# Two-block transformer on one core: recurrence outputs in another PSUM bank, decay moved onto the keys, masked diagonal copies, and sparse-attention operands loaded two heads earlier

## The chip, the cores and the metric

The program runs on one core of a Trainium2 chip. A core has five engines with a queue each: TensorE (PE, with its weight loads as PEld), VectorE (DVE), ScalarE (ACT), GpSimd (POOL) and SyncE (SP), which here issues nearly all DMAs. Each queue runs in the order in which the program put the instructions. The metric is device time in microseconds (us), the median of several executions.

## The reference

512 tokens of width 1024 pass two blocks in float32. Block 1 is attention over two blocks of 256 tokens with a causal mask and a distance bias, a pooling branch and an MLP. Block 2 has a mixer with two branches: an RWKV-7 recurrence and a sparse attention (NSA) with 16 query heads in 4 groups. A gate merges the branches; cross attention and a convolutional MLP follow. Two pieces matter here:

```python
def step(state, inp):                       # rwkv7_scan, 16 heads of 64
    r_t, w_t, k_t, v_t, a_t, b_t = inp
    sa = jnp.einsum('bhvk,bhk->bhv', state, a_t)
    state = state * w_t[:, :, None, :] + sa[..., None] * b_t[:, :, None, :] + v_t[..., None] * k_t[:, :, None, :]
    return state, jnp.einsum('bhvk,bhk->bhv', state, r_t)
...
out = gb[..., 0:1] * o_c + gb[..., 1:2] * o_s + gb[..., 2:3] * o_w    # NSA: compressed, selected, window
```

## The kernel before, in words

All matrices are kept with features on partitions and 512 tokens along the free axis. A float32 product is made of three passes over operands split into a high and a low part (lines 242 to 244), or of plain float32 matmuls, which the profile shows as two records each.

The part that the change touches is the stage between the projections and the merge of the two branches, from about 1050 to 1530 us of the span. `emit` weaves three instruction streams there (`weave`, with the weights 190, 240 and 65 for their pace), and a scheduler then fixes the order on every engine:

- stream "" is `nsa`: 4 groups, each with a prologue (load the group's queries, keys and bias, split them, scores against the compressed keys at L1124, a softmax over them, lines 1125 to 1147) and then 4 heads with two branches each through `attend` (scores L307/L308, exponentials L311, scaling L317/L319, transposes L324, evictions L326/L327, products L328/L329).
- stream "_b" is `rwkv_backs`: for 8 pairs of heads, `rwkv_operands` prepares a pair (keys transposed at L827 and copied to `L3` at L828, values at L833, inverse blocks at L843 and L849) while `rwkv_chain` walks the 8 chunks of 64 tokens of the pair before it, and `rwkv_finish` normalises its output.
- stream "_m" is `merge_gates`: 10 column tiles of a projection (buffer `psg_m`), with 512 KB weight tiles loaded at L208, split at L221 and L222, and sent to memory by POOL at L954.

A step of `rwkv_chain` is a sequence of dependent pieces, each of two heads on the diagonal of a 128x128 block. In one PSUM bank, tile `p` (`psb_b` in the profile) has four blocks of 128 columns: the state against the chunk (`p[:, 1]`, L868), copied by DVE to `RH` (L870, one copy for each head); the output of the chunk before (`p[:, 0]`, L873 and L875), copied by ACT to `Y` (L877); the solved values (`p[:, 2]`, L882), copied by DVE to `VU` (L884); the state's increment (`p[:, 3]`, L886), which DVE adds to the decayed state (L893), where ACT has put state times decay ahead of it (L892). The bank has one buffer, and waits are kept for the tile as a whole.

`ld` is a pool of three 128x512 buffers through which the sparse attention loads values, keys, queries and the compressed bias (L292, L1100, L1110, L1115); `f` has three buffers as well, `kb` one, and PSUM bank 5 (`psa_b`) serves `rwkv_operands` alone.

Of the kernel before, what the change touches and what calls it, by code (L numbers as in the profile page):

```python
# [38 lines left out]
class Gen:  # L39
# [248 lines left out]
    def k_stack(self, k, par):  # L288

        t = self.f("ld")  # L290
        for b in range(2):
            self.nc.sync.dma_start(t[64 * b:64 * b + 64], k[64 * par:64 * par + 64])  # L292
        return self.split(t, tag="kst")
# [327 lines left out]
    def rwkv_state(self):  # L621
# [6 lines left out]
        self.ne, self.et = (zero(n, 512).rearrange("p (c t) -> p c t", c=4) for n in ("ne", "et"))  # L628
        self.cen = zero("cen", 128)
# [163 lines left out]
    def rwkv_operands(self, pr):  # L793
# [29 lines left out]

        for q in range(2):
# [31 lines left out]
    def rwkv_chain(self, pr, out, L3, VS, VU, YI):  # L856
# [8 lines left out]
        for c in range(9):  # L865
            p = self.ps("b").rearrange("p (e n) -> p e n", e=4)
            if c < 8:
                nc.tensor.matmul(p[:, 1], fl(L1[:, c]), fl(VS[:, c]), start=True, stop=True)  # L868
                for a in H:
                    V.tensor_copy(RH[a, a], p[a, 1, a])  # L870
            if c:

                nc.tensor.matmul(p[:, 0], fl(VU[:, c - 1]), L4[:, :, c - 1], start=True, stop=c == 1)  # L873
                if c > 1:
                    nc.tensor.matmul(p[:, 0], fl(VS[:, c - 1]), self.rb[:, :, c - 1], start=False, stop=True)  # L875
                for a in H:
                    S.copy(Y[a, c - 1], p[a, 0, a])  # L877
# [5 lines left out]
            for h, a in enumerate(H):  # L883
                V.tensor_copy(VU[a, c, h], p[a, 2, a])  # L884
            if c < 7:
                nc.tensor.matmul(p[:, 3], L3[:, c], fl(VU[:, c]), start=True, stop=True)  # L886
                d = self.decay[:, pr, c:c + 1]
                for h, a in enumerate(H):
                    if c == 0:
                        V.tensor_scalar(VS[a, 1, h], p[a, 3, a], d[a], None, op0=OP.mult)  # L890
                    else:
                        S.activation(VS[a, c + 1, h], VS[a, c, h], AF.Copy, scale=d[a])  # L892
                        V.scalar_tensor_tensor(VS[a, c + 1, h], p[a, 3, a], d[a], VS[a, c + 1, h], OP.mult, OP.add)  # L893
# [140 lines left out]
    def nsa(self):  # L1034

        nc, A, V, S = self.nc, self.A, self.nc.vector, self.nc.scalar
        for gp in range(2):
            yield from self.nsa_groups(gp, *self.cmp)

# [54 lines left out]
    def nsa_groups(self, gp, kc, vc):  # L1094
# [9 lines left out]
        for gl in range(2):  # L1104
            g = 2 * gp + gl
            kst = {br: self.k_stack(self.kvd[2 + 2 * br + gp], gl) for br in (1, 2)}
            qst = {}
            for i in range(2):
                q = self.f("ld")
                nc.sync.dma_start(q, self.qd[2 * g + i])  # L1110
                for par in range(2):
                    qst[2 * i + par] = self.q_stack(q, par, -0.125)

            cb = self.f("ld")
            nc.sync.dma_start(cb, bass.AP(tensor=self.gfd.tensor, offset=self.gfd.offset + 4 * g * 1056 + 513,  # L1115
# [477 lines left out]
```

## Time and profile before

| | |
|---|---|
| median of 3 runs | 2163.73 us (2156.9 to 2164.24) |
| the profiled execution's own time | 2160.68 us |
| its span, first to last instruction | 2158.9 us |
| instructions | 28062 |
| busy PE / PEld / DVE / ACT / POOL | 2040.6 / 1640.7 / 1333.7 / 957.7 / 64.1 us |
| mean granted TensorE clock | 0.969 |
| HBM traffic | 205.12 MB read, 45.53 MB written |

PE is called busy for 95% of the span. A share over the span hides that the stages differ: in the dense products PE runs without a gap, and in the woven stage it doesn't. A row of the waits names the engine and line that stood idle, and the engine and line that ended the wait; the three numbers are the sum, the count and the longest. The granted clock is 1.00 at 2.4 GHz and 0.50 at 1.2 GHz; a stretch in between had both.

### The profile page before, as it was taken

Reading aid. Unit: us, or ns where it says so; the run is one execution under the profiler, and the core shown is the slowest. Engines: PE = TensorE matmul, PEld = TensorE weight load, DVE = VectorE, ACT = ScalarE, POOL = GpSimd, SP = SyncE. Lnnn points to the kernel's source line nnn. Section 1 sums busy time; section 2 is a strip of 40 time slices with the busy share of each in tenths; the row PEclk is TensorE's granted clock in tenths of the full one; section 3 lists DMA queues with packets and bytes.
Section 4 is the critical chain, followed back from the end, with each engine's and each line's share of the span. In section 5 each row is a group of like instructions: output and inputs, shape, how many; then the busy total and the mean of one; then the engine's idle time right before and its main releaser. Section 6 shows DMA issues by size and latency. Waiting matters only on the chain.

```text
span 2158.9 us, 28062 instructions
## 1 busy us (share of the span) xinstructions
PE 2040.6 (95%) x9927; PEld 1640.7 (76%) x9927; DVE 1333.7 (62%) x3111; ACT 957.7 (44%) x1874; POOL 64.1 (3%) x131
## 2 busy tenths in 40 slices
PE   8999999999999999899888997887999999999999
PEld 7777888888887778677676776665778878888887
DVE  5785433553556576969388877775656766666522
ACT  4864422442343243333376776765424443333311
POOL 0000000000011201000000000000000000000000
PEclk9999999999999999999999998997999999999999
DMA  4233233333465756455544544351543122333332
GB/s 160 74 93 97 89 98 94 116 109 121 130 203 157 175 149 167 146 147 165 167 106 115 137 115 114 101 157 59 161 151 89 59 69 88 98 98 90 98 113 81
DMA packets 172493, 256.71 MB, mean 119 GB/s; under 512 B 87200, under 2 KB 102768, under 8 KB 172352
## 3 DMA queue, kind: packets, MB, share of 16 engines
q1 hardware_dynamic: 169024, 244.42, 38.8%
q0 software_dynamic: 3328, 10.49, 1.4%
q8 instruction: 79, 1.29, 0.3%
q14 instruction: 62, 0.51, 0.1%
HBM read 205.12 MB, written 45.53 MB: 116 GB/s over the span
## 4 chain that ended last, share of the span: by engine, by line
PE 43%; DVE 7%; DMA 5%; ACT 3%; issue 1%; SPq 0%; ACTq 0%; DVEq 0%
PE psg L244 8%; PE psg L242 8%; PE psg L243 8%; PE psg_b L243 1%; PE psg_b L244 1%; PE psg_b L242 1%; DMA bias<-grd 1%; DVE ys L772 1%; DMA ws<-in_w_in 1%; PE psg_p L242 1%; PE psb L324 1%; PE psg_p L243 1%; PE psg_p L244 1%; DMA ld<-qd 1%; PE psa L739 1%
## 5 line engine op out<-in xcount | busy, mean ns | idle before, releaser
L221 ACT CAST wh<-ws 128x1024 fp32r<-128x1024 f32 (+2 forms) x283 | 291.5, 1031 | 707.3 <-PE psg L243 461.1
L222 DVE TENSOR_TENSOR wl<-ws,wh 128x1024 fp32r<-128x1024 f32 (+2 forms) x283 | 340.2, 1203 | 275.1 <-ACT wh L221 269.8
L242 PE MATMUL psg<-xh,wh 128*128 128x512 f32 x984 | 392.8, 399 | 4.6 <-ACT wh L221 4.6
L244 PE MATMUL psg<-xh,wl 128*128 128x512 f32 x984 | 393.7, 400 | 0.0
L243 PE MATMUL psg<-act,wh 128*128 128x512 f32 x912 | 360.3, 395 | 1.1 <-DVE act L165 1.1
L242 PEld LDWEIGHTS psg<-xh,wh 128*128 128x128 f32 x984 | 186.0, 189 | 46.7 <-ACT wh L221 5.4
L244 PEld LDWEIGHTS psg<-xh,wl 128*128 128x128 f32 x984 | 186.1, 189 | 41.9 <-issue 1.2
L243 PEld LDWEIGHTS psg<-act,wh 128*128 128x128 f32 x912 | 171.5, 188 | 43.0 <-DVE act L165 1.5
L242 PE MATMUL psg<-act,wh 128*128 128x512 f32 x496 | 196.6, 398 | 2.8 <-ACT act L164 1.4
L244 PE MATMUL psg<-act,wl 128*128 128x512 f32 x496 | 196.7, 397 | 0.5 <-DVE wl L222 0.5
L243 PE MATMUL psg<-xl,wh 128*128 128x512 f32 x352 | 139.7, 397 | 0.0
L242 PEld LDWEIGHTS psg<-act,wh 128*128 128x128 f32 x496 | 93.2, 188 | 27.4 <-ACT act L164 2.2
L244 PEld LDWEIGHTS psg<-act,wl 128*128 128x128 f32 x496 | 93.4, 188 | 23.9 <-DVE wl L222 1.3
L311 ACT ACTIVATE p<-p,sm 128x128 f32<-128x128 f32 (+3 forms) x160 | 89.5, 560 | 18.1 <-DVE sm L309 16.7
L243 PE MATMUL psg<-x,wh 128*128 128x512 f32 x216 | 88.9, 412 | 0.0
L327 DVE TENSOR_TENSOR pt<-psb,pt 128x512 fp32r<-128x512 f32 (+3 forms) x160 | 76.4, 489 | 19.3 <-ACT pt L326 16.2
L324 PE MATMUL psb<-ident,p 128*128 128x128 f32 x400 | 80.8, 293 | 2.9 <-DVE y L917 1.2
L309 DVE CUSTOM_DVE_ANT_0 p<-psa,bias 128x128 f32<-128x128 f32 (+3 forms) x160 | 76.0, 487 | 11.4 <-PE psa L308 4.9
L326 ACT CAST pt<-psb 128x512 fp32r<-128x512 f32 (+3 forms) x160 | 66.2, 423 | 33.9 <-PE psb L324 31.1
L243 PEld LDWEIGHTS psg<-xl,wh 128*128 128x128 f32 x352 | 66.2, 188 | 14.3
L242 PE MATMUL psg_p<-xh,wh 128*128 128x512 f32 x176 | 72.8, 414 | 0.8 <-ACT f L953 0.6
L243 PE MATMUL psg_p<-x,wh 128*128 128x512 f32 x176 | 72.3, 411 | 0.0
(485 smaller groups left out, 3944.4 us busy)
## 6 DMA issues: line engine op xcount, KB each, us to landing
ws<-in_w_in SPq DMA_DIRECT2D x59, 512.0 KB, 4.3
ws<-in_w_fup SPq DMA_DIRECT2D x44, 512.0 KB, 3.4
ws<-in_w_up SPq DMA_DIRECT2D x32, 512.0 KB, 3.6
ws<-in_w_down SPq DMA_DIRECT2D x32, 512.0 KB, 3.6
ws<-in_w_fdn SPq DMA_DIRECT2D x16, 512.0 KB, 3.5
ws<-in_w_qku SPq DMA_DIRECT2D x12, 512.0 KB, 3.3
ws<-in_w_out SPq DMA_DIRECT2D x8, 512.0 KB, 3.6
ws<-in_w_cak SPq DMA_DIRECT2D x8, 512.0 KB, 4.3
```

Of the source, the lines that this page charges most:

```text
L221: nc.scalar.copy(wh[:, :n], ws[:, :n])
L222: nc.vector.tensor_tensor(wl[:, :n], ws[:, :n], wh[:, :n].bitcast(F32), OP.subtract)
L242: nc.tensor.matmul(p[:, :n], wh[:, s], h[:, :n], start=c + k == 0, stop=False)
L243: nc.tensor.matmul(p[:, :n], wh[:, s], l[:, :n], start=False, stop=False)
L244: nc.tensor.matmul(p[:, :n], wl[:, s], h[:, :n], start=False, stop=last)
L309: nc.vector.tensor_tensor_reduce(pt, ps[:, :w], bias[:, 512 - w:], 1.0, 3e38, OP.add, OP.min, m[:, i:i + 1])
L311: nc.scalar.activation(pt, pt, AF.Exp, bias=m[:, i:i + 1], scale=-1.0, accum_out=s[:, i:i + 1])
L324: nc.tensor.transpose(ps[:, (i - j) * 128:(i - j + 1) * 128], P[i][:, j * 128:j * 128 + 128], self.ident)
L326: nc.scalar.copy(ph[:, :w], ps[:, :w])
L327: nc.vector.tensor_tensor(pl[:, :w], ps[:, :w], ph[:, :w].bitcast(F32), OP.subtract)
L739: nc.tensor.matmul(p[:, c], KB[hs, 4 * q + c].rearrange("p e t -> p (e t)"), AR[hs, :, 4 * q + c], start=True, stop=True)
L772: V.tensor_tensor(q, a, Y[:, :n, :t + 1], OP.mult)
```

## The change

- `rwkv_chain` writes the output of the chunk before into a tile of its own from `self.ps("a")`, which for this stream is bank 5, and ACT copies `Y` from there.
- The two DVE copies for the heads become one `copy_predicated` over 128 columns, for `RH` and for `VU`; the mask `diag` is the block matrix `blk` read as integers.
- `rwkv_operands` multiplies the keys `KB` (128x1024) by the decay of their chunk on POOL, ahead of the transposes. The product of L886 then comes out decayed, ACT's multiplication (L892) is gone, and one DVE instruction for each head makes state times decay plus increment.
- `nsa_loads` takes the loads of a group's two query tiles, its compressed bias (now in an `f` buffer) and the keys of its first branch out of the prologue. For groups 1 to 3 it is called when the third head of the group before begins (`h == 2`), for group 0 at the start. The keys of the second branch and the values are loaded where they were.

```diff
--- before.py
+++ after.py
@@ -285,12 +285,15 @@
         nc.vector.scalar_tensor_tensor(st[b], q[a], scale, st[a].bitcast(F32), OP.mult, OP.subtract)
         return st
 
-    def k_stack(self, k, par):
-
+    def k_load(self, k, par):
         t = self.f("ld")
         for b in range(2):
             self.nc.sync.dma_start(t[64 * b:64 * b + 64], k[64 * par:64 * par + 64])
-        return self.split(t, tag="kst")
+        return t
+
+    def k_stack(self, k, par):
+
+        return self.split(self.k_load(k, par), tag="kst")
 
     def attend(self, qst, kst, bias, V, o, first, last, gate=None):
 
@@ -626,6 +629,7 @@
         self.yi = [zero(f"yi{i}", 1024).rearrange("p (c h t) -> p c h t", c=8, h=2) for i in range(2)]
         self.rh = zero("rh", 128)
         self.ne, self.et = (zero(n, 512).rearrange("p (c t) -> p c t", c=4) for n in ("ne", "et"))
+        self.diag = self.blk.rearrange("p a b -> p (a b)").bitcast(I32)
         self.cen = zero("cen", 128)
         for t in (*self.yi, self.rh, self.ne, self.et, self.cen):
             nc.gpsimd.memset(t, 0.0)
@@ -821,6 +825,7 @@
             nc.gpsimd.memset(VS[64 * h:64 * h + 64, 0, h], 0.0)
         yield 1.0
 
+        nc.gpsimd.tensor_tensor(KB, KB, self.decay[:, pr][:, :, None].to_broadcast([128, 8, 128]), OP.mult)
         for q in range(2):
             p = self.ps("a")
             for c in range(4):
@@ -866,31 +871,29 @@
             p = self.ps("b").rearrange("p (e n) -> p e n", e=4)
             if c < 8:
                 nc.tensor.matmul(p[:, 1], fl(L1[:, c]), fl(VS[:, c]), start=True, stop=True)
+                V.copy_predicated(RH, self.diag, p[:, 1])
+            if c:
+
+                o = self.ps("a")
+                nc.tensor.matmul(o[:, :128], fl(VU[:, c - 1]), L4[:, :, c - 1], start=True, stop=c == 1)
+                if c > 1:
+                    nc.tensor.matmul(o[:, :128], fl(VS[:, c - 1]), self.rb[:, :, c - 1], start=False, stop=True)
                 for a in H:
-                    V.tensor_copy(RH[a, a], p[a, 1, a])
-            if c:
-
-                nc.tensor.matmul(p[:, 0], fl(VU[:, c - 1]), L4[:, :, c - 1], start=True, stop=c == 1)
-                if c > 1:
-                    nc.tensor.matmul(p[:, 0], fl(VS[:, c - 1]), self.rb[:, :, c - 1], start=False, stop=True)
-                for a in H:
-                    S.copy(Y[a, c - 1], p[a, 0, a])
+                    S.copy(Y[a, c - 1], o[a, a])
             if c in (4, 8) and pr < 7:
                 self.rwkv_load(pr + 1, c // 8)
             if c == 8:
                 break
             nc.tensor.matmul(p[:, 2], fl(YI[:, c]), RH, start=True, stop=True)
-            for h, a in enumerate(H):
-                V.tensor_copy(VU[a, c, h], p[a, 2, a])
+            V.copy_predicated(fl(VU[:, c]), self.diag, p[:, 2])
             if c < 7:
                 nc.tensor.matmul(p[:, 3], L3[:, c], fl(VU[:, c]), start=True, stop=True)
                 d = self.decay[:, pr, c:c + 1]
                 for h, a in enumerate(H):
                     if c == 0:
-                        V.tensor_scalar(VS[a, 1, h], p[a, 3, a], d[a], None, op0=OP.mult)
+                        V.tensor_copy(VS[a, 1, h], p[a, 3, a])
                     else:
-                        S.activation(VS[a, c + 1, h], VS[a, c, h], AF.Copy, scale=d[a])
-                        V.scalar_tensor_tensor(VS[a, c + 1, h], p[a, 3, a], d[a], VS[a, c + 1, h], OP.mult, OP.add)
+                        V.scalar_tensor_tensor(VS[a, c + 1, h], VS[a, c, h], d[a], p[a, 3, a], OP.mult, OP.add)
             yield 1.2
         g, bv = self.f("vgb"), self.f("vgb")
         nc.sync.dma_start(g, self.vgd[pr, 1])
@@ -1034,8 +1037,21 @@
     def nsa(self):
 
         nc, A, V, S = self.nc, self.A, self.nc.vector, self.nc.scalar
+        self.ahead = self.nsa_loads(0)
         for gp in range(2):
             yield from self.nsa_groups(gp, *self.cmp)
+
+    def nsa_loads(self, g):
+
+        nc = self.nc
+        qs = []
+        for i in range(2):
+            qs.append(self.f("ld"))
+            nc.sync.dma_start(qs[i], self.qd[2 * g + i])
+        cb = self.f("f")
+        nc.sync.dma_start(cb, bass.AP(tensor=self.gfd.tensor, offset=self.gfd.offset + 4 * g * 1056 + 513,
+                                      ap=[[1056, 4], [-16, 32], [1, 512]]))
+        return qs, cb, self.k_load(self.kvd[4 + g // 2], g % 2)
 
     def nsa_compressed(self):
         nc, A, V, S = self.nc, self.A, self.nc.vector, self.nc.scalar
@@ -1103,17 +1119,10 @@
             V.tensor_tensor(v[:, :, :, 64:128], z, v[:, :, :, 0:64].bitcast(F32), OP.subtract)
         for gl in range(2):
             g = 2 * gp + gl
-            kst = {br: self.k_stack(self.kvd[2 + 2 * br + gp], gl) for br in (1, 2)}
-            qst = {}
-            for i in range(2):
-                q = self.f("ld")
-                nc.sync.dma_start(q, self.qd[2 * g + i])
-                for par in range(2):
-                    qst[2 * i + par] = self.q_stack(q, par, -0.125)
-
-            cb = self.f("ld")
-            nc.sync.dma_start(cb, bass.AP(tensor=self.gfd.tensor, offset=self.gfd.offset + 4 * g * 1056 + 513,
-                                          ap=[[1056, 4], [-16, 32], [1, 512]]))
+            qs, cb, k1 = self.ahead
+            qst = {2 * i + par: self.q_stack(qs[i], par, -0.125) for i in range(2) for par in range(2)}
+            kst = {1: self.split(k1, tag="kst"), 2: self.k_stack(self.kvd[6 + gp], gl)}
+
             kz = self.f("kz", F32R, (128, 448)).rearrange("p (i n) -> p i n", i=2)
             nc.gpsimd.memset(kz.bitcast(F32), 0.0)
             for i, k in enumerate(kc):
@@ -1153,6 +1162,8 @@
                 par = h % 2
                 if par == 0:
                     O = self.f("o")
+                if h == 2 and g < 3:
+                    self.ahead = self.nsa_loads(g + 1)
                 bias = self.f("bias")
                 nc.sync.dma_start(bias, bass.AP(tensor=self.grd.tensor, offset=self.grd.offset + hd * 1280 + 127,
                                                 ap=[[576, 2], [-1, 64], [1, 512]]))
```

The scheduler orders the three streams anew. PE at the last chunks of the eighth pair, in the kernel before (`psb_b` is the chain's bank, `kst` keys, `pt` transposed probabilities):

```order
L329 MATMUL pso_13328<-pt_13534,vt_11591 128x512
L324 MATMUL psb_13549<-ident,p_13501 128x128 x2
L868 MATMUL psb_b_13307<-vs_12580,ws_9002 128x128
L873 MATMUL psb_b_13307<-wh_9003,vu_12581 128x128
L875 MATMUL psb_b_13307<-rb,vs_12580 128x128
L882 MATMUL psb_b_13307<-rh,yi_5055 128x128
L886 MATMUL psb_b_13307<-vu_12581,bk_12579 128x128
L868 MATMUL psb_b_13397<-vs_12580,ws_9002 128x128
L873 MATMUL psb_b_13397<-wh_9003,vu_12581 128x128
```

The same place in the changed kernel (`psa_b` is bank 5, `psg_m` the merge gates; L873, L887 and L890 are the former L868, L882 and L886):

```order
L873 MATMUL psb_b_13248<-vs_12474,ws_9002 128x128
L332 MATMUL pso_13179<-pt_13243,vt_11521 128x128
L311 MATMUL psa_13431<-kst_12750,qst_12743 128x256
L310 MATMUL psa_13436<-kst_12749,qst_12743 128x384
L311 MATMUL psa_13436<-kst_12750,qst_12743 128x384
L887 MATMUL psb_b_13248<-rh,yi_5055 128x128
L244 MATMUL psg_m_13630<-xh_4697,wl_13634 128x512
L310 MATMUL psa_13441<-kst_12749,qst_12743 128x512
L327 MATMUL psb_13376<-ident,p_13349 128x128
L890 MATMUL psb_b_13248<-vu_12475,bk_12473 128x128
L878 MATMUL psa_b_13264<-wh_9003,vu_12475 128x128
```

Before, the chain's matmuls of these chunks follow each other; now matmuls of the attention and of the gates stand between them, and the output (L878) comes behind the chain's last matmul of the step.

SP at the loads of the third group, in the kernel before (`yi`, `vu`, `ynd` are other streams' transfers):

```order
L811 DMA yi_5055<-ydr 32x8x32 x4
L1110 DMA ld_11624<-qd 128x512
L838 DMA vu_11444<-vs_11443 64x8x64
L1171 DMA ynd<-o_11042 128x512
L1115 DMA ld_11632<-gfd 128x1x512
```

and in the changed kernel:

```order
L1050 DMA ld_10980<-qd 128x512
L1050 DMA ld_10982<-qd 128x512
L899 DMA vgb_10803<-vgd 128x512
L923 DMA yrd<-y_9671 128x512
L900 DMA vgb_10804<-vgd 128x512
L1052 DMA f_10984<-gfd 128x1x512
L291 DMA ld_10986<-kvd 64x512 x2
L1168 DMA bias_10989<-grd 128x1x512
```

Both query tiles, the compressed bias and the first keys now stand together, ahead of the bias of the group before's third head (the last row).

POOL in the changed kernel, from the third group's prologue on:

```order
L1127 MEMSET kz_11555 128x448
L828 TENSOR_TENSOR kb_10816<-kb_10816,decay 128x1024
L957 DMA zmd<-f_10674 128x512
L825 MEMSET vs_10820 64x64 x2
L828 TENSOR_TENSOR kb_11370<-kb_11370,decay 128x1024
```

The TENSOR_TENSOR rows, one for each pair, are new; before, this queue had the memsets and the gates' DMAs alone.

## Rows read from the trace of the kernel before

**Rows 1.** The page, part 2: 40 equal slices, tenths of PE busy, then of granted clock.
```profile
PE   8999999999999999899888997887999999999999
...
PEclk9999999999999999999999998997999999999999
```

**Rows 2.** Windows: stretch, length, busy PE, PEld, DVE, ACT, POOL (instructions), clock, DMA share, GB/s.
```profile
1050.00:1530.00 480.00, 405.99 (x2176) 316.83 (x2175) 357.39 (x1209) 317.30 (x883) 11.80 (x33) 0.90 0.42 116
1050.00:1070.00 20.00, 10.61 (x43) 8.05 (x42) 8.10 (x13) 7.96 (x16) 2.59 (x8) 0.80 0.43 140
...
1320.00:1340.00 20.00, 13.23 (x63) 10.90 (x62) 11.11 (x41) 11.92 (x33) 0.00 (x0) 0.74 0.43 114
...
1470.00:1500.00 30.00, 16.89 (x62) 12.56 (x61) 12.11 (x45) 8.41 (x25) 0.00 (x0) 0.58 0.20 59
...
1680.00:2150.00 470.00, 467.38 (x2086) 375.87 (x2085) 263.10 (x402) 160.75 (x226) 0.00 (x0) 1.00 0.29 89
```

**Rows 3.** Waits of PE from 1055 to 1527 us: sum, times, longest.
```profile
PE psb_b L882 <- ACT y L877: 23.2, 14, 6.9
PE psa L1124 <- DVE qst L285: 6.6, 2, 6.1
...
PE psb L1128 <- DVE ld L1125: 3.7, 2, 1.9
...
PE psb_b L873 <- DVE rh L870: 3.5, 6, 0.8
```

**Rows 4.** Waits of ACT in the same stretch.
```profile
ACT qst L284 <- DMA ld<-qd: 11.0, 3, 5.9
ACT wh L221 <- DMA ws<-in_w_in: 7.8, 2, 6.7
```

**Rows 5.** Timeline, start and duration, at PE's three longest waits for L877.
```profile
1320.68 1.18 SPq L1110 DMA_DIRECT2D ld<-qd  x2
...
1330.72 0.63 ACT L284 ACTIVATE qst<-ld 64x512 fp32r<-64x512 f32 x1 [5.89 <-DMA ld<-qd]
...
1331.51 0.42 ACT L877 COPY y<-psb_b 64x64 f32<-64x64 f32 x2
...
1331.98 0.80 PE L882 MATMUL psb_b<-rh,yi 128*128 128x128 f32 x2 [6.10 <-ACT y L877]
...
1179.89 0.49 PE L882 MATMUL psb_b<-rh,yi 128*128 128x128 f32 x2 [3.38 <-ACT y L877]
...
1379.59 0.79 PE L882 MATMUL psb_b<-rh,yi 128*128 128x128 f32 x2 [6.85 <-ACT y L877]
```

**Rows 6.** Timeline of one step of the chain in the stage's last part.
```profile
1474.93 0.71 PE L868 MATMUL psb_b<-vs,ws 128*128 128x128 f32 x2 [0.79 <-DVE vs L893]
...
1476.21 0.80 PE L873 MATMUL psb_b<-wh,vu 128*128 128x128 f32 x2 [0.57 <-DVE rh L870]
...
1477.47 0.42 ACT L877 COPY y<-psb_b 64x64 f32<-64x64 f32 x2 [2.27 <-PE psb_b L875]
...
1477.94 0.80 PE L882 MATMUL psb_b<-rh,yi 128*128 128x128 f32 x2 [0.51 <-ACT y L877]
...
1480.85 0.77 PE L868 MATMUL psb_b<-vs,ws 128*128 128x128 f32 x2 [0.77 <-DVE vs L893]
```

**Rows 7.** Groups by line and shape: count, busy us, mean ns, idle before and its causes.
```profile
L870 DVE COPY rh<-psb_b 64x64 f32<-64x64 f32 x128 | 28.2, 221 | 10.4 <-PE psb_b L868 8.0
...
L327 DVE TENSOR_TENSOR pt<-psb,pt 128x128 fp32r<-128x128 f32 x32 | 9.2, 288 | 1.9 <-ACT pt L326 1.4
...
L892 ACT ACTIVATE vs<-vs,decay 64x64 f32<-64x64 f32 x96 | 33.0, 343 | 21.1 <-DVE vs L893 13.2 <-DVE vs L890 6.7
```

**Rows 8.** Timeline of POOL's arithmetic in an earlier stage and of DVE beside it.
```profile
714.29 6.23 POOL L999 TENSOR_TENSOR blk<-src,pev 64x248 f32<-64x248 f32 x8
...
714.06 0.24 DVE L1016 TENSOR_SCALAR f<-f 128x128 f32<-128x128 f32 x1 [4.74 <-ACT f L1015]
...
715.16 0.75 DVE L1016 TENSOR_SCALAR f<-f 128x128 f32<-128x128 f32 x1
```

## The prediction

> **What bounds the kernel.** I read the slices of the page first. PE is busy in nine tenths or more nearly everywhere, but the granted clock falls below nine tenths in only one slice, and both are weakest about two thirds through [rows 1]. The windows then say what that is worth. From 1680 to 2150 us PE is busy for 467.4 of 470 us at clock 1.00: nothing but less PE work could shorten that stage, and the change touches none of it. From 1050 to 1530 us PE is busy for only 406.0 of 480 us, at clock 0.90 [rows 2]. So 480 - 406.0 = 74 us are idle, and of the busy time about 406.0 x 0.10 = 41 us are lost to the lower clock: some 115 us that are not PE work. DVE (357 of 480) and ACT (317 of 480) aren't full either. The change leaves PE's work as it is, so it can only win from these 115 us.
>
> Next, the waits of PE in that stretch [rows 3]. The largest group is L882 waiting for ACT's copy of the outputs, L877: 23.2 us in 14 waits. L882 doesn't need that copy. It writes another quarter of the tile that L877 reads, and the wait is on the tile. The timeline shows why it gets long [rows 5]: ACT's queue runs in order, and at 1330.72 it had stood 5.89 us at L284, whose query tile was issued by SP at 1320.68 and came 10 us later. L877 stood behind it, and L882, and everything behind that on PE: 6.10 us. The wait of 3.38 us at 1179.89 is the same story; ACT's waits for query tiles are 11.0 us in all [rows 4]. The one of 6.85 us at 1379.59 stands on another load, the gates' weight tile (ACT 6.7 us, L221), which the change doesn't move. The two prologue waits (L1124 for the split queries 6.6 us, L1128 for the bias sum 3.7 us [rows 3]) come from the same loads.
>
> Last, the chain by itself: one step is 1480.85 - 1474.93 = 5.92 us, and in it PE has L873 at 1476.21 and can start L882 only at 1477.94, when ACT is done [rows 6]. From 1470 to 1500 us almost nothing stands beside the chain: PE is busy 16.9 of 30 us at clock 0.58 [rows 2].
>
> **The change, part by part.** The sum is made against the profiled execution's 2160.68 us (span 2158.9).
>
> *Loads ahead.* What they can remove is 6.10 + 3.38 [rows 5] + 6.6 + 3.7 [rows 3] = 19.8 us of idle PE. Group 0 is loaded at the same place as before; its queries only come first in the queue, before the values, and no longer wait for an `ld` buffer. So I take all of 6.10 and 3.38, 1.8 of the second L1128 wait, and half of the 6.1 at L1124: 14 us. Bounds 0 (the next late thing ends the same gaps) and 19.8. SP issues these DMAs anyway; five transfers for a group are moved past the third head's bias, which costs that bias their issue time, half of 1.18 us each [rows 5], with most of a head to hide it. The cover is the third and fourth head's work.
>
> *A bank of its own.* Of the 23.2 us, 6.10 and 3.38 are counted above; 13.7 are left, half of them the wait on the weight tile. There PE gets a few chain matmuls further and then stands at the next instruction that needs ACT. I take 5 us, bounds 0 and 13.7. The added wait: an output now waits for ACT's copy of the previous output, a whole step earlier, and for the operands' copies out of bank 5.
>
> *The last chunks.* In the order of the changed kernel other streams' matmuls stand between the chain's. The window shows 30 - 16.9 = 13.1 us idle and 16.9 x 0.42 = 7.1 us lost to the clock: 20 us in all, the upper bound; the lower is 0. The chain's step also loses the 1477.94 - 1476.21 = 1.73 us behind L873. I take three quarters, 15 us, since the pieces there are the ones that the order rows show filled.
>
> *The clock elsewhere.* After the waits of rows 5 the clock is down: 13.2 x 0.26 = 3.4 us in 1320 to 1340, 10.6 x 0.20 = 2.1 us in 1050 to 1070 [rows 2]. I take 5 us, bounds 0 and 10.
>
> *Work taken from ACT and DVE.* ACT loses 96 x 343 ns = 33 us (L892). DVE loses 256 copies of 221 ns (56 us, L870 and its twin L884) and gets 128 masked copies of 128 columns. Such a copy isn't in the trace. It can't be faster than one of the copies that it replaces, 221 ns, and I bound it above by two passes of the two-input form of 128 columns, 2 x 288 ns; I take 288 ns, since it too has an input from PSUM and one from SBUF [rows 7]: 37 us, 20 less. Neither engine is full in this stage, so I count nothing for it, 0 to 10 us.
>
> *Keys on POOL.* Eight passes over 1024 columns. A pass over 248 columns takes 6.23 / 8 = 0.78 us [rows 8]; a longer one takes no less, and by columns 4.1 x 0.78 = 3.2 us, which I take. That is 26 us on an engine that is busy 11.8 of 480, for a pair that the chain reaches some 50 us later (480 us for eight pairs and the ends), so its own time is hidden. It isn't free for DVE: beside POOL's passes the same DVE instruction took 0.75 instead of 0.24 us [rows 8]. The Trainium skill (SBUF — State Buffer, section Who interferes with whom) says why: DVE's second port pair is shared with GpSimd, and the one that comes second stands until the other is done. The trace agrees: 0.75 is about one pass of POOL. By that rule each of the eight passes can hold DVE once for up to 3.2 us, 26 us in all if each fell on the path. I take 5 us lost, bounds 0 and 26, because the chain's own DVE instructions mostly read PSUM and at most one operand from SBUF.
>
> *New order.* Four us lost to waits that the new order makes, bounds 0 and 45 (below).
>
> Sum: 14 + 5 + 15 + 5 - 5 - 4 = 30 us, so 2160.68 - 30 = 2130.7 us. The median of the runs shown, 2163.73, stands 3 us above the profiled execution; for a median of the changed kernel I predict **2134 us**.
>
> **Rivals.**
> 1. *The next late thing.* ACT still meets weight tiles, the heads' biases and the second branch's keys, none of which is loaded earlier. If these end the gaps of rows 5, only the last chunks are left, with 10 to 15 us: about 2150. For it: 6.7 of ACT's waits are a weight tile [rows 4]. Against it: the query tiles are the larger share.
> 2. *POOL in the way.* All eight passes hold DVE where the chain needs it: 30 + 5 - 26 = 9 us gained, about 2155. Against it: a step's DVE work is short beside 3.2 us, and the streams beside it can run on.
> 3. *The shared bank, slower.* Bank 5 had 6 operand tiles for a pair; now 8 output tiles go through it too, one buffer for all, and PE can't write one until ACT or DVE has read the one before. Where ACT is late, PE stands at the output matmul as it stood at L882. At 0.7 us for each of 64 steps this is 45 us: 2163.7 - 30 + 45 = 2179, slower. It decides from 30 / 64 = 0.47 us for a step, and passes the bound for slower at 0.64. The Trainium skill (PSUM — Partial Sum Buffer, section on bank collisions) says that engines must be kept apart by bank and quadrant, not by address; the trace agrees, since L882 waits for a copy of other columns, 23.2 us in all, and the rule holds for bank 5 as well. Against it: PE's waits for the chain's DVE copies, L873 for L870, are 3.5 us in six waits [rows 3], and an output has a whole step of 5.92 us for its eviction.
> 4. *All gaps close.* With the chain shortened by 1.73 of 5.92 us in every step and the clock kept up, some 60 of the 115 us could go: 2104.
> 5. *The change doesn't do what it says.* The loads stand earlier in SP's order, but SP runs in order too; behind a blocked transfer they come no earlier. That ends as rival 1.
>
> **How the numbers follow.** A measurement of this kernel can tell about 0.5% (10.8 us) from no change, so faster is below 2152.9 and slower above 2174.5. Forecast (2118 to 2152) 0.56; rivals 1 and 5 together 0.13, half of it still faster; rival 2 0.08, a third of it faster; rival 3 0.09, of which 0.08 beyond the bound; rival 4 0.14. Faster: 0.56 + 0.14 + 0.06 + 0.03 = 0.79; slower 0.08; the same 0.13. The range reaches from rival 4's better half to rivals 1 and 2: 2100 to 2160, with about 0.07 below and 0.12 above.
>
> **What would show it.** Right: no group L887 <- ACT among PE's waits; the waits of L284 for queries near 0 instead of 11.0; the stretch of the last chunks at clock above 0.9; a masked copy near 0.29 us; POOL's pass near 3.2 us; the stage shorter by about 30 us and the stages beside it unchanged. The loads' term is wrong if ACT still stands at L284; the bank's, if the output matmuls L878 appear among PE's waits on ACT with over 20 us; the last chunks', if PE is idle there as long as before. A masked copy of 0.6 us, or DVE instructions stretched to 3 us beside POOL in numbers, would speak for rival 2.

## The result: faster by 2.5%, more than forecast

| | before | changed |
|---|---|---|
| median | 2161.17 us | 2104.59 us (2102.59 to 2105.07) |
| ratio to before, 95% interval | | 0.9747 [0.9729, 0.9765] |
| span of the profiled execution | 2158.9 us | 2103.3 us |
| instructions | 28062 | 27840 |
| mean granted clock | 0.969 | 0.976 |

The forecast was 2134 us, some 30 us less than before. The kernel became 55.6 us shorter in the profiled span: inside the range, in the forecast's direction, but almost twice its size. It is the 2104 us of the rival "all gaps close".

The slices of the changed kernel answer to [rows 1]. From the twentieth slice on, seven had stood at eight or seven tenths of PE busy; now four do, all at eight. The granted clock was below nine tenths in two slices (the prediction read one), and now is in four, all at eight tenths.

```profile
PE   8999999999999999899988889999999999999999
...
PEclk9999999999999999899988899999999999999999
```

The windows of the changed kernel (columns as in [rows 2]). The stage starts at 1050 us as before. Its end is set 628.9 us ahead of the span's end in both kernels, at 1474.4 instead of 1530; the last row, shifted by as much, holds the same work.

```profile
1050.00:1474.40 424.40, 376.46 (x2161) 304.26 (x2160) 328.27 (x1078) 282.85 (x783) 26.32 (x37) 0.92 0.46 130
1050.00:1070.00 20.00, 10.62 (x41) 6.68 (x39) 12.92 (x20) 8.35 (x15) 3.12 (x5) 0.75 0.55 154
...
1414.40:1444.40 30.00, 26.61 (x161) 21.08 (x158) 24.59 (x77) 19.43 (x51) 1.08 (x2) 0.97 0.58 189
1444.40:1474.40 30.00, 29.71 (x151) 24.00 (x152) 25.72 (x72) 25.39 (x64) 0.00 (x0) 0.92 0.50 149
1624.40:2094.40 470.00, 467.41 (x2086) 375.60 (x2086) 262.98 (x402) 160.60 (x226) 0.00 (x0) 1.00 0.29 89
```

Against [rows 2] the stage is 480 - 424.4 = 55.6 us shorter, which is all of the gain. Of that, 74.0 - 47.9 = 26.1 us are idle time of PE, and 406.0 - 376.5 = 29.5 us are busy time, although PE's matmuls are the same (9927 in either page). The stretch before the stage's last 30 us, 16.9 us busy at clock 0.58 before, is now 26.6 us busy at 0.97. The first 20 us gained nothing. The last row, the later stage, is unchanged.

PE's waits in the stage (1055 to 1472 us), which answer to [rows 3]:

```profile
PE psg_m L242 <- ACT wh L221: 8.4, 2, 7.1
PE psb L1156 <- DVE f L1153: 6.9, 1, 6.9
PE psg_m L242 <- ACT f L956: 4.4, 1, 4.4
...
PE psb_b L873 <- DVE vs L896: 2.5, 4, 1.3
...
PE psa_b L878 <- DVE vs L842: 1.4, 1, 1.4
...
PE psb_b L887 <- DVE rh L874: 1.2, 3, 0.4
```

The solve matmul (L887, before L882) no longer waits for ACT; that was 23.2 us. The output matmuls (L878) don't take its place: the largest of their waits is 1.4 us. What is left is a weight tile (L221) and the first group's softmax (L1153).

ACT's waits in the same stretch, against [rows 4]: no row of L284 for query tiles is left, where 11.0 us were; the weight tiles cost 12.2 us instead of 7.8.

```profile
ACT y L882 <- PE psa_b L880: 18.3, 20, 3.3
...
ACT wh L221 <- DMA ws<-in_w_in: 12.2, 3, 6.5
```

Groups by line and shape (columns as in [rows 7]): a masked copy takes 297 ns, POOL's pass over the keys 1.96 us on average.

```profile
L896 DVE SCALAR_TENSOR_TENSOR vs<-vs,decay,psb_b 64x64 f32<-64x64 f32 x96 | 26.7, 279 | 16.5 <-PE psb_b L890 15.1
...
L874 DVE COPY_PREDICATED rh<-blk,psb_b 128x128 f32<-128x128 int32 x64 | 19.0, 297 | 12.3 <-PE psb_b L873 11.7
L888 DVE COPY_PREDICATED vu<-blk,psb_b 128x128 f32<-128x128 int32 x64 | 19.0, 297 | 9.6 <-PE psb_b L887 8.7
...
L828 POOL TENSOR_TENSOR kb<-kb,decay 128x1024 f32<-128x1024 f32 x8 | 15.7, 1962 | 96.4 <-DMA kb<-kbd 81.5 <-PE pso L331 14.9
```

The timeline of one step near the chain's end, against [rows 6]:

```profile
1424.36 0.38 PE L873 MATMUL psb_b<-vs,ws 128*128 128x128 f32 x2
1424.78 0.31 DVE L874 COPY_PREDICATED rh<-blk,psb_b 128x128 f32<-128x128 int32 x1 [0.24 <-PE psb_b L873]
...
1425.38 0.39 PE L887 MATMUL psb_b<-rh,yi 128*128 128x128 f32 x2
...
1426.49 0.39 PE L878 MATMUL psa_b<-wh,vu 128*128 128x128 f32 x2
...
1427.69 0.46 PE L873 MATMUL psb_b<-vs,ws 128*128 128x128 f32 x2
...
1427.79 0.41 ACT L882 COPY y<-psa_b 64x64 f32<-64x64 f32 x2
```

From state matmul to state matmul it is 1427.69 - 1424.36 = 3.33 us, where the step shown before took 5.92. It is one of the shortest: the median of the 63 intervals went from 5.84 to 4.74 us. The output (L878) runs beside the state's update, and ACT copies it when the next step has begun.

### The profile page after: what moved, and what is told of

It is laid out like the page before. It is cut to its first block, busy times and chain, and to the rows that moved or that the text cites. A ratio compares the mean times of both kernels' runs of the same rounds, so it can differ in the third digit from the quotient of the medians.

```text
span 2103.3 us, 27840 instructions
## 1 busy us (share of the span) xinstructions
PE 2013.3 (96%) x9927; PEld 1629.6 (77%) x9927; DVE 1306.4 (62%) x2983; ACT 925.7 (44%) x1778; POOL 80.0 (4%) x139
## 4 chain that ended last, share of the span: by engine, by line
PE 47%; DVE 5%; ACT 4%; DMA 3%; issue 1%; SPq 1%; DVEq 0%; ACTq 0%
PE psg L242 8%; PE psg L243 8%; PE psg L244 8%; DMA ws<-in_w_in 2%; PE psg_b L242 1%; PE psg_b L243 1%; PE psg_b L244 1%; PE psb L327 1%; PE psg_p L242 1%; PE psg_p L243 1%; PE psg_p L244 1%; PE pso L331 1%; PE psa L743 1%; DVE ys L776 1%; PE pso L332 1%
## 5 line engine op out<-in xcount | busy, mean ns | idle before, releaser
L221 ACT CAST wh<-ws 128x1024 fp32r<-128x1024 f32 (+2 forms) x283 | 291.5, 1031 | 708.0 <-PE psg L243 461.5
L329 ACT CAST pt<-psb 128x512 fp32r<-128x512 f32 (+3 forms) x160 | 65.5, 425 | 34.5 <-PE psb L327 31.0
```

The lines of the kernel that those rows point to most:

```text
L221: nc.scalar.copy(wh[:, :n], ws[:, :n])
L329: nc.scalar.copy(ph[:, :w], ps[:, :w])
```

## The experiments

Each ratio is to the kernel before, measured beside it; 0.01 is 21.6 us.

**One part alone, then all but one.** Three theories stood at the start. A: each part pays by itself, and the terms of the sum were too small. B: the parts pay only together, or share a gain. C: it is the order that the scheduler happens to find, which any edit changes. The edits are the hunks of the diff above: the tile `o` (bank), `copy_predicated` with `diag` (mask), POOL's pass with the shorter state update (keys), `nsa_loads` (loads).

```diff
 one_bank, added to the kernel before; no_bank, taken from the changed one
+                o = self.ps("a")
+                    S.copy(Y[a, c - 1], o[a, a])
 one_mask, no_mask
+                V.copy_predicated(RH, self.diag, p[:, 1])
+            V.copy_predicated(fl(VU[:, c]), self.diag, p[:, 2])
 one_keys, no_keys
+        nc.gpsimd.tensor_tensor(KB, KB, self.decay[:, pr][:, :, None].to_broadcast([128, 8, 128]), OP.mult)
+                        V.scalar_tensor_tensor(VS[a, c + 1, h], VS[a, c, h], d[a], p[a, 3, a], OP.mult, OP.add)
 one_loads, no_loads
+        self.ahead = self.nsa_loads(0)
+                    self.ahead = self.nsa_loads(g + 1)
```

> The kernel before with the first part alone: the outputs' tile in bank 5, copies, decay and loads as before. Theory A (each part has a worth of its own, the forecast's terms only undersized): 10 to 20 us less than before, and the wait of PE's L882 for ACT's output copy (23.2 us) gone from the list. Theory B (the parts pay only together: with the queries still loaded late, ACT stands and PE meets it at its next instruction): 0 to 7 us less. Theory C (any part deals the order of the streams anew, and the gain is that deal's luck): anywhere from 15 us less to 15 us more, without regard to which wait is gone.

> The kernel before with the masked copies alone. A: 0 to 8 us less, as DVE loses some 18 us of work (256 x 0.221 against 128 x 0.297) of which little is on the path. B: nothing, within 5 us. C: 15 us either way.

> The kernel before with the keys decayed on POOL alone (ACT's 96 multiplications of 343 ns gone). A: 0 to 10 us less, since ACT's work is off the path for the most part and POOL's eight passes of 1.9 us hold DVE now and then. B: within 5 us. C: 15 us either way.

> The kernel before with the loads two heads ahead alone. A: 14 to 20 us less, ACT's waits of L284 for query tiles down from 11.0 us to below 2. B: 5 to 10 us less, since PE's L882 keeps waiting for ACT's output copy wherever ACT stands on something else. C: 15 us either way.

> The changed kernel with the outputs back in the chain's own tile; everything else of the change stays. A, each part by itself (the bank alone gave 36 us, the masked copies alone 29): 2105 + 36 = 2141 us, PE again idle at the solve matmul behind ACT's copy of the outputs, and the sparse stretch near the stage's end is back. B, both shorten the same step and share the gain: the bank is worth less once the masked copies are in, 10 to 20 us, so 2115 to 2125. C, the order that the scheduler happens to find: anywhere from 2105 to 2160, with no more waits at the solve matmul than the one part predicts.

> The changed kernel with the two DVE copies for the heads in place of each masked copy. A: 2105 + 29 = 2134 us. B: 2115 to 2120, since the own bank already takes the longest waits of the step away. C: anywhere from 2105 to 2160. DVE's busy time should be up by about 20 to 27 us in every case.

> The changed kernel without POOL's pass over the keys; ACT multiplies the state by the decay again. A: keys alone gave nothing, so 2104 to 2106 us, no difference. B, with the chain shortened, ACT's 33 us of multiplications now stand in its way: 2112 to 2120. C: anywhere from 2095 to 2125.

> The changed kernel with a group's loads back in its prologue. A: the loads alone gave nothing, so 2104 to 2107 us. B, with the other waits gone the 10 us of ACT's wait for query tiles are no longer covered: 2112 to 2120, with ACT's wait for the queries back among its largest. C: anywhere from 2095 to 2125.

| part | alone | all but it | bought alone | lost when left out |
|---|---|---|---|---|
| bank | 0.9833 [0.9811, 0.9855] | 0.9852 [0.9826, 0.9877] | 36 us | 23 us |
| mask | 0.9866 [0.9847, 0.9884] | 0.9836 [0.9815, 0.9857] | 29 us | 19 us |
| keys | 1.0005 [0.9991, 1.002] | 0.9763 [0.973, 0.9795] | -1 us | 3 us |
| loads | 0.999 [0.9971, 1.0008] | 0.978 [0.9758, 0.9802] | 2 us | 7 us |

Bank and mask carry the gain, each with far more than any of the theories had allowed alone (10 to 20 us for the bank, 0 to 8 for the mask). Without one of them the time (2130.74 and 2128.68 us) lies between what A and B expected, so they share a part of it. Without the keys or the loads it is 2111.99 and 2116.64 us, at the lower end and within what B expected; the paces below decide that. That the loads alone bought nothing is what the forecast least allowed for. The windows of the kernel with the loads alone say how:

```profile
1050.00:1530.00 480.00, 415.32 (x2177) 322.89 (x2177) 357.29 (x1209) 317.57 (x883) 12.27 (x34) 0.88 0.41 116
```

PE's idle time did fall, from 74.0 to 64.7 us, and ACT's wait for query tiles was gone. But PE was busy 9.3 us longer for the same matmuls, at clock 0.88 instead of 0.90 (415.3 x 0.12 = 49.8 us lost to the clock, where 40.6 had been), and the stage ended at the same time. PE's idle time was not what bound it.

**What binds the stage: the chain.** A view of one line gives the first and the last start of the chain's state matmul. For the kernel before, and for the changed one:

```profile
L868 PE MATMUL psb_b<-vs,ws x128: 270/275/553, 1073.5 to 1481.2; 128*128 128x128 f32 x128
```
```profile
L873 PE MATMUL psb_b<-vs,ws x128: 270/275/582, 1076.1 to 1430.9; 128*128 128x128 f32 x128
```

The 63 intervals took 1481.2 - 1073.5 = 407.7 us, now 354.8: 52.9 us less, and the span is 55.6 less. The same row in the other runs (us; the difference is the span without the chain):

| kernel | chain | span | difference |
|---|---|---|---|
| before | 407.7 | 2158.9 | 1751 |
| one_keys | 408.2 | 2161.0 | 1753 |
| one_loads | 403.8 | 2158.9 | 1755 |
| one_bank | 378.5 | 2121.7 | 1743 |
| one_mask | 374.2 | 2127.4 | 1753 |
| no_mask | 374.3 | 2126.8 | 1753 |
| no_bank | 372.2 | 2127.4 | 1755 |
| no_loads | 365.5 | 2114.9 | 1749 |
| no_keys | 358.2 | 2105.6 | 1747 |
| changed | 354.8 | 2103.3 | 1749 |

The chain's time differs by 53 us over these ten kernels, the rest by 12. So theory D: the chain's 63 dependent steps set the stage's end, and an edit is worth what it takes out of a step, times 63, whether or not its engine is full. (The chain isn't the last to end: the attention's last product comes some 40 us behind it. The runs at other paces, below, show how the two hang together.) That they go together doesn't show which drives which. Two runs put the same sort of work on DVE, once in the chain and once beside it.

```diff
 chain_copy: the changed kernel
                 V.copy_predicated(RH, self.diag, p[:, 1])
+                V.tensor_copy(RH[H[0], H[0]], p[H[0], 1, H[0]])
...
             V.copy_predicated(fl(VU[:, c]), self.diag, p[:, 2])
+            V.tensor_copy(VU[H[0], c, 0], p[H[0], 2, H[0]])
 side_copy: the changed kernel
             nc.tensor.matmul(p[:, 2], fl(YI[:, c]), RH, start=True, stop=True)
+            V.tensor_reduce(self.f("scr", shape=(128, 16))[:, :1], self.ident, AX.X, OP.add)
...
                 nc.tensor.matmul(p[:, 3], L3[:, c], fl(VU[:, c]), start=True, stop=True)
+                V.tensor_reduce(self.f("scr", shape=(128, 16))[:, :1], self.ident, AX.X, OP.add)
```

> The changed kernel with one more DVE copy of 64x64 behind each of the 128 masked copies, onto the same place, so that the next matmul of the chain waits for it (the values stay the same). D, the chain of 63 steps sets the stage's end (in ten traces the span is about 1750 us plus the time from the chain's first step to its last): 128 x 0.22 = 28 us, so 2104 + 28 = 2132, chain time 355 + 28 = 383 us. E, DVE's load sets it: 28 us of work on an engine that is busy 328 of 424 us, 5 to 10 us, as much as the next run. C, the scheduler's luck: no relation to the copies, anywhere from 2100 to 2130.

> The changed kernel with 120 more DVE instructions in the chain's steps for which nothing waits: a sum over 128 columns of a constant (about 0.25 us) into a scratch column, issued behind the solve and increment matmuls. Some 30 us of DVE work as in the run beside it, but off the chain. D: 2104 to 2112 us, chain time up by 0 to 8 us. E: as much as the run beside it. C: anywhere from 2100 to 2130.

chain_copy: 2137.28 us, ratio 0.9897 [0.9864, 0.9929], which is 32 us behind the change. side_copy: 2097.04 us, 0.9702 [0.9677, 0.9726], 10 us ahead of it. The added work by line and shape, first of chain_copy, then of side_copy:

```profile
L890 DVE COPY vu<-psb_b 64x64 f32<-64x64 f32 x64 | 13.3, 208 | 0.4
L875 DVE COPY rh<-psb_b 64x64 f32<-64x64 f32 x64 | 13.3, 207 | 0.2
```
```profile
L888 DVE TENSOR_REDUCE scr<-ident 128x1 f32<-128x128 f32 x58 | 16.0, 276 | 0.4
L892 DVE TENSOR_REDUCE scr<-ident 128x1 f32<-128x128 f32 x50 | 13.9, 278 | 0.5
```

The chain's row of chain_copy, then of side_copy:

```profile
L873 PE MATMUL psb_b<-vs,ws x128: 270/275/553, 1075.8 to 1457.5; 128*128 128x128 f32 x128
```
```profile
L873 PE MATMUL psb_b<-vs,ws x128: 270/275/553, 1076.9 to 1421.6; 128*128 128x128 f32 x128
```

In the chain, 26.6 us of copies made the chain 381.7 - 354.8 = 26.9 us longer, and the 32 us in time are more than any change of order alone brought (27, below). Beside it, 29.9 us in the records shown made nothing longer; the chain even became 10 us shorter, 344.7 us, and the span with it. DVE's load (theory E) falls: it isn't how full DVE is that counts. D holds, apart from side_copy's gain, which it did not expect. At 2097 us side_copy is the fastest kernel of all, with work that nobody needs. That a better order came with it is likely, but no run shows it.

**Why the own bank pays.** The output could leave the step's middle, or the bank itself could be what counts. late_out moves the output behind the increment and leaves it in the chain's tile.

```diff
 late_out: the kernel before, in rwkv_chain
-                nc.tensor.matmul(p[:, 0], fl(VU[:, c - 1]), L4[:, :, c - 1], start=True, stop=c == 1)
...
-                    S.copy(Y[a, c - 1], p[a, 0, a])
...
             nc.tensor.matmul(p[:, 2], fl(YI[:, c]), RH, start=True, stop=True)
...
+                nc.tensor.matmul(p[:, 0], fl(VU[:, c - 1]), L4[:, :, c - 1], start=True, stop=c == 1)
...
+                    S.copy(Y[a, c - 1], p[a, 0, a])
```

> The kernel before with the output of the chunk before written at the end of the step, behind the increment, but still in the chain's own tile (no other bank). F, the own bank pays because the solve no longer has the output matmuls and ACT's copy ahead of it: most of its 36 us comes here too, 2120 to 2140 us, state to solve down from 3.4 us to about 2.4, solve no longer waiting for ACT. G, the bank itself pays, since one tile for all ties the chain to ACT wherever the output stands: here the next step's first matmul waits for ACT's copy instead, the step keeps its length, 2150 to 2165 us.

2158.27 us, 0.9991 [0.9973, 1.001]: nothing. By the starts of the matmuls in the timeline, over the 56 steps that are followed by one of the same pair, the mean time from state to solve fell from 3.40 to 1.99 us, as F expected, but that from the increment to the next state rose from 1.50 to 2.95; the chain took 407.5 us. PE's waits name the new place:

```profile
PE psb_b L868 <- ACT y L889: 8.2, 18, 1.7
```

F falls and G holds: as long as one tile serves for everything, ACT's copy stands in the chain's way, wherever it is put. With the tile `o`, the copy may end a step later.

The state matmul's starts show where that pays, and it is mostly not in the step. Of the 63 intervals 56 lie within a pair of heads, and seven lead from a pair's last chunk to the next pair's first. From the kernel before to one_bank the 56 went from 357.9 to 352.6 us, the seven from 49.5 to 25.7: 24 of the 29 us that the chain lost. In the kernel before, each pair's first state matmul starts 0.1 to 0.2 us behind ACT's copy of the last output of the pair before it; in one_bank each starts ahead of that copy. At the eighth pair, the kernel before, then one_bank:

```profile
1438.88 0.42 ACT L877 COPY y<-psb_b 64x64 f32<-64x64 f32 x2 [1.06 <-PE psb_b L875]
...
1439.50 0.68 PE L868 MATMUL psb_b<-vs,ws 128*128 128x128 f32 x2
```
```profile
1416.87 0.39 PE L868 MATMUL psb_b<-vs,ws 128*128 128x128 f32 x2
...
1417.07 0.42 ACT L878 COPY y<-psa_b 64x64 f32<-64x64 f32 x2
```

late_out leaves that copy ahead of the next pair (45.9 us for the seven). With the masked copies in, it is the same: from one_mask to bank_mask (the run with bank and mask, below) the seven fell from 43.2 to 25.5 us, the 56 not at all (330.7 and 333.4). Only between no_bank and the changed kernel do the 56 carry the difference (337.0 to 321.9), as two passages of the changed kernel took 11.9 and 6.6 us. Within a pair, what the mean step of one_bank won from state to solve (0.95 us) it nearly lost again behind the solve (0.85 us); why, no run tells.

The shared bank 5 has its price too, and it is small; in one_bank the largest wait on it is

```profile
PE psa_b L827 <- ACT y L878: 3.0, 3, 2.0
```

**How much is the order's luck.** side_copy gained 10 us by more work, so C isn't empty. The runs below change the recurrence's pace in the weave, one number in `emit`, for three kernels: before, before with bank and mask (bank_mask), and changed.

```diff
-  ("_b", right(), 240)
+  ("_b", right(), 225)    or 260
```

> The kernel before with one number changed: the recurrence's pace in the weave is 260 instead of 240, so its instructions are written a little earlier among the other streams'. No instruction is added or taken away. D: a step's length is set by its own dependent pieces, so the chain's 408 us can fall only by what it waits behind other streams, 0 to 20 us: 2140 to 2162. C, the order alone: a change as large as the parts', 20 us or more either way.

> The changed kernel with the recurrence's pace at 260 instead of 240. D: the chain's 355 us fall or rise by little, 2095 to 2110. C: 2090 to 2130. In both cases its distance to the run beside it says whether the gain of 56 us hangs on one lucky order: by D it stays 40 to 60 us, by C it can be anything.

> The kernel before with the outputs' own bank and the masked copies, without the decayed keys and the earlier loads. D, the chain alone: these two parts are all that shortens it, 2105 to 2118 us, chain time 355 to 370 us. B, the loads and the keys pay once the chain is short: the run without the loads was 7 us and the run without the keys 3 us behind the change, so 2115 to 2120 us or more if they help each other. An order's luck is worth some 10 us either way.

> The changed kernel with the recurrence's pace at 225 instead of 240. At 260 the chain took 347 us (8 less) but the attention ended later and the time was 15 us longer, so the stage ends with whichever of the two streams is late. If so, at 225 the chain is longer, 360 to 375 us, and ends the stage: 2105 to 2125 us. If at 240 it is still the attention that is late: 2095 to 2103 us.

> The kernel before with the recurrence's pace at 225. At 260 it took the same as at 240. If the chain's own pieces bind it, the order hardly matters here too: 2150 to 2170 us, and the change's gain at 225 is some 40 us. If before sits on an unlucky order at 240: below 2145 us.

> Own bank and masked copies alone, with the recurrence's pace at 225; stands beside the whole change at 225, 2121 us. If the loads and the decayed keys pay, it is 6 us or more behind it, 2127 to 2135; if they are worth nothing apart from the order that they bring, 2110 to 2125.

> The same at 260; the whole change took 2120 us there. If the loads and the decayed keys pay: 2126 to 2135 us; if they are worth nothing: 2105 to 2124.

| pace | before | bank and mask | whole change |
|---|---|---|---|
| 225 | 1.0062 [1.0041, 1.0083] | 0.9767 [0.9729, 0.9805] | 0.9822 [0.9797, 0.9848] |
| 240 | 1 | 0.977 [0.9736, 0.9804] | 0.9747 [0.9729, 0.9765] |
| 260 | 0.9991 [0.9972, 1.0009] | 0.9892 [0.9861, 0.9923] | 0.9807 [0.978, 0.9833] |

The change gains at every pace: by the ratios of the columns 2.4, 2.5 and 1.8%, 49 us on average. With the order alone its own time moves by 16 us and that of bank and mask by 27, more than D had allowed for (2095 to 2110 us at 260; it took 2119.64). So the 56 us are the best of three paces, some 7 above their average. Loads and keys together, the whole change against bank and mask, are worth -12, +5 and +18 us at the three paces: not told apart from the order. The rule "1750 us plus the chain" holds within one pace only: at 260 the changed kernel's chain took 347.0 us, 7.8 less than at 240, and its span was 11.9 us longer. The traces show why. In this table each cell has the kernel before, bank and mask, and the whole change; the products are those of the 256 of the attention (buffer `pso`, L328 and L329 before) that start behind the chain's last state matmul:

| pace | chain, us | from its last step to the attention's last product, us | products behind it |
|---|---|---|---|
| 225 | 435.9 / 370.7 / 367.1 | 29.3 / 27.2 / 28.5 | 22 / 24 / 24 |
| 240 | 407.7 / 359.0 / 354.8 | 43.2 / 40.4 / 42.5 | 38 / 40 / 40 |
| 260 | 396.5 / 370.0 / 347.0 | 60.7 / 65.0 / 62.1 | 54 / 56 / 57 |

The attention is the last to end in every kernel, and by how much depends on the pace, hardly on the chain's length. PE's queue holds both streams in one order. The counts fit a simple account, though no run tests it by itself: what stands behind a step of the chain comes sooner when the step is shorter, and the pace sets how much is left behind the last step. So at 260 the kernel before has a chain 11.2 us shorter than at 240 and the same time. At 240 bank and mask came as D expected (chain 355 to 370 us), and so did the changed kernel's chain at 225 (360 to 375). At each pace the change shortens the chain (by 68.8, 52.9 and 49.5 us); the span without the chain still differs by 12 to 15 us among the kernels of one pace, and what is worth less than that can't be read from the chain.

## Why the prediction was too small, point by point

- **What bounds the stage.** Here it failed: "it can only win from these 115 us", and each edit was then priced by the waits of PE that it would end. The stage was bound by the chain. An idle time of PE counts only as far as it holds up the chain, and a piece of the chain counts although it shows as no wait of PE. Even busy time of PE gave way: half of the gain (29.5 us) is busy time, while the clock of the stage rose only from 0.90 to 0.92, worth 40.6 - 30.1 = 10 us by the forecast's own rule. Why the same matmuls are busy some 20 us less beyond that, no run here tells.
- **Work taken from ACT and DVE: 0, measured 19 to 29 us** (mask left out, mask alone). This is the largest miss. The duration was right (288 ns taken, 297 measured). The step that failed is "Neither engine is full in this stage, so I count nothing for it". The chain stands still while these copies run: with the 288 ns that the prediction took, 2 x (2 x 221 - 288) = 0.31 us for a step, 63 times, would have been 19 us from rows that it had.
- **A bank of its own: 5, measured 23 to 36 us.** The mechanism was right in that the wait on the tile is gone; the size was taken from PE's 13.7 us of idle time. The 1.73 us behind L873 were seen, but only used for the last chunks and in rival 4. The prediction had no term for the seven passages from pair to pair, where 24 of the 29 us lie that one_bank's chain lost.
- **The last chunks: 15.** The stretch is gone, as its sign said (clock 0.97). It isn't a term of its own: the chain ended late because each step was long. With the masked copies alone a stretch of 19.2 us busy in 30 at clock 0.62 remained, and 29 us were gained all the same.
- **The clock elsewhere: 5, measured about 4.** Of the 10 us above, 7.1 - 26.6 x 0.03 = 6.3 are the last chunks'. In the first 20 us, one of the two places named, the clock fell from 0.80 to 0.75.
- **Loads ahead: 14, measured 2 alone, 7 when left out,** both within the order's spread. ACT's wait for queries went from 11.0 us to nothing, as said, but these gaps weren't what the chain waited for most.
- **Keys on POOL: -5, measured -1 and +3.** The pass took 1.96 us, not 3.2. DVE is held by it, as the prediction said, in four of the eight passes; in three of them a piece of the chain stood behind the held instruction, for some 3 us in all (below).
- **New order: -4.** It is no loss with a bound of 45 us but a spread: 15 us over three paces for the kernel before, 16 for the changed one.
- **Rivals.** PE's waits on the shared bank come to some 3 us where 45 were priced: it falls. The loads did come earlier, so rival 5 falls too. POOL in the way: falls at 1.96 us a pass. The next late thing: the weight tile does stand first among PE's waits now (8.4 us), but it doesn't set the end. "All gaps close" gave 2104 us for a reason half right: it was the one case that counted a shorter step everywhere. But 47.9 us of gaps are still there, the mean step lost 52.9 / 63 = 0.84 us and not 1.73 (which, 63 times, would be 109 us), so that its hit on the number is luck.

## What to carry to other kernels

Where one stream of dependent steps runs beside others, look first for its first and last start and count its steps: an edit inside a step is worth its saving times the number of steps, even on an engine that is far from full, and a gap closed outside the chain can be worth nothing (here 2 of 2160 us). Look at the passages from one run of steps to the next as well. To learn which it is, add a known amount of work once inside the chain and once beside it. And where a scheduler orders the streams, take a part's gain at two or three paces before believing one of less than some 20 us.

## What the runs showed of the hardware

A masked copy of 128 columns from PSUM takes 297 ns, 1.34 times one of the two 64-column copies that it replaces (221 ns, [rows 7]).

POOL's pass over 1024 columns takes 1.96 us on the mean where one over 248 (on half the partitions) took 0.78 [rows 8]: four times the columns take 2.5 times as long. While it runs, some DVE instructions stand still. Timeline of the changed kernel at three passes:

```profile
1063.13 1.89 POOL L828 TENSOR_TENSOR kb<-kb,decay 128x1024 f32<-128x1024 f32 x1 [5.20 <-DMA kb<-kbd]
1063.29 1.77 DVE L1151 TENSOR_TENSOR sm<-sm,gt 128x16 f32<-128x16 f32 x1
...
1253.06 2.12 POOL L828 TENSOR_TENSOR kb<-kb,decay 128x1024 f32<-128x1024 f32 x1 [18.00 <-DMA kb<-kbd]
1253.45 0.29 DVE L896 SCALAR_TENSOR_TENSOR vs<-vs,decay,psb_b 64x64 f32<-64x64 f32 x1
1253.77 0.42 DVE L312 CUSTOM_DVE_ANT_0 p<-psa,bias 128x256 f32<-128x256 f32 x1
...
1334.32 0.43 PE L887 MATMUL psb_b<-rh,yi 128*128 128x128 f32 x2
...
1334.51 1.89 POOL L828 TENSOR_TENSOR kb<-kb,decay 128x1024 f32<-128x1024 f32 x1 [14.87 <-PE pso L331]
1334.53 2.22 DVE L322 TENSOR_SCALAR p<-p,sm 128x128 f32<-128x128 f32 x2
...
1336.67 0.28 DVE L888 COPY_PREDICATED vu<-blk,psb_b 128x128 f32<-128x128 int32 x1
```

A product of 16 columns with both inputs in SBUF took 1.77 us and ended with POOL's pass; instructions that read one input from PSUM, as the chain's do, ran at their usual length beside another pass. The Trainium skill (SBUF — State Buffer, section Who interferes with whom) states just this: DVE contends with a reading GpSimd instruction when it has two inputs in SBUF, and whoever comes second stands until the other is done. The trace agrees, with 1.77 us for the one and 0.29 us for the other.

At the third pass shown an instruction with one tensor and a column of scalars in SBUF was held as well: the first of the two L322 took 1.96 us, where 0.28 is their median. And an instruction that isn't held itself stands behind one that is, since DVE's queue runs in order: the chain's solve (L887) was done at 1334.75, and its masked copy (L888) began at 1336.67. At two more passes the state's update stood behind an L317 of 1.45 us (median 0.16) and an L776 of 0.90 (median 0.18). From 1.96 - 0.28, 1.45 - 0.16 and the half microsecond that the third cost, the estimate is some 3 us of the chain for the eight passes.
